# Query and key high/low parts: made at the input projection instead of inside the attention

## The chip, the cores and the metric

The kernel runs on one core of a Trainium2 chip. The metric is the device time of one execution in microseconds (us); the median of several runs is given.

## The reference, cut to what matters

One layer of a hybrid decoder trunk on 512 positions, width 2048. After an RMS norm, one projection `z = a @ w_in` feeds two groups of heads: a gated linear recurrence (RG-LRU) and a sparse attention (NSA) with 16 query heads in 4 key/value groups. Their outputs are normalised, projected by `w_out`, and followed by an MLP and a gated embedding. The part that the change touches:

```
q (512,16,64), k_s and k_w (512,4,64) = columns of z
s = q . k * 64**-0.5 + bias          (selected and window branch, and q . kc for the compressed branch)
p = softmax(s);  o = p . v           (three branches, summed with sigmoid gates)
```

All inputs and outputs are float32.

## The kernel before, in words

**Products in parts.** TensorE multiplies rounded operands (type fp32r). To keep float32 accuracy each operand x is split into a high part h (x rounded, a copy on ScalarE, ACT) and a low part x - h (a subtraction on VectorE, DVE), and a product is three matmuls: high by high, high by low, low by high (`mm3`, L165). The scores take two matmuls, one with the keys' high and one with their low part (L1226, L1227, L1233, L1234). A query tile `al_q` holds for one head the high part of the 64 query dimensions in one half of the 128 partitions and the low part in the other half; the key tiles `kh` and `kl` hold the same 64 dimensions in both halves, so one matmul gives two of the partial products.

**Strips and order.** The work is a list of strips. A strip is 512 columns of a weight tile: four weight blocks of 128 columns, so 12 matmuls. `go` (L188) walks the list once and writes out every engine's instructions in that order: at strip j it makes the high and low part of the weights of strip j + 4 (`split`, lines L159 on ACT and L160 on DVE, from a `raw` buffer that a DMA filled), hands out up to two finished results, and issues the matmuls of strip j. Everything else is hung on a strip position by hand with `at` (in quarters of a strip). Each engine executes its instructions in that order, and so do the DMA issues of each queue: loads are issued by SP, stores by ACT (`store`, L422).

**The input projection** (`front`, L560). 16 pairs of weight tiles in the order kc, vc, k0, k1, 0 to 5, q0, 6, 7, q1, q2, q3. Each pair takes 16 strips (k0 and k1 take eight extra strips of the compression). `proj` (L697) evicts each of the two results of a pair (L701, DVE, 128x512) into a tile `z`; the pairs 0 to 7 stay on chip for the recurrence (`lru_tile`), the others are stored to `z_d` in DRAM, one DMA of 512 KB each. The tiles `z` come from a ring of three buffers (`z_tile`, L241), so a tile waits until the third tile before it has been read. q0 belongs to the heads of group 0, q3 to those of group 3, k0 to groups 0 and 1, k1 to groups 2 and 3.

**The attention** (`mid`, L975; `attention`, L1068; `group`, L1077; `head`, L1206). It runs between the 32 strips of the first half of `w_out`: a step at position s of the attention's own scale is hung at strip b2 + 2 + 0.165 s, where b2 is the first of these strips. Group g starts at B = 11 + 27 g and head r of it at B + 6.75 r; `GA`, `GQ`, `HA`, `HBI` and the like hold the offsets. Before its scores a group prepares:

- `load` (L1087): SP loads the keys twice, into the lower and the upper partitions (L1090, 256 KB each), and the queries (L1092, 512 KB) into two buffers of the `raw` ring of five, which the weight strips use too
- `q_turn` (L1104): DVE scales the queries by -0.125 and reverses the order of positions (L1107, two of 128x512)
- `q_hi`, `q_lo` (L1109, L1113): per head, ACT makes the high part (L1111, 64x512) and DVE the low part (L1115, 64x512)
- `k_hi`, `k_lo` (L1117, L1121): ACT (L1119) and DVE (L1122), 128x1024 each
- `kc_hi`, `kc_lo` (L1124, L1128): the same for the compressed keys, in four small pieces

`c_score` (L1142) is the group's first use of its queries on TensorE (L1145, L1146). In a head, `score(qt)` (L1218) writes into one of two PSUM banks, and `bias(qt)` (L1237, line L1241 on DVE) reads it, adds the bias and takes the minimum, which frees the bank; then follow the exponential (L1246, ACT), a scaling on GpSimd (L1256), transposes (L1266), the split of the transposed probabilities (L1278, L1282) and the products with the values (L1293). The sum of a head is read out by `out_a` and `out_b` (L1308, L1315), which frees the one bank of the output product (L1299).

**At the seam.** `switch2` (L994) reopens the z ring with one buffer, which lies over the buffer that the last tile of the front had used, and clears two constant tiles (`attn_const`, L1061: L1064 and L1066 on DVE). The first results of `w_out` go into that buffer (`y1_out`, L981: L985 on DVE).

Of the kernel before, what the change touches and what calls it, by code (L numbers as in the profile page):

```python
# [9 lines left out]
F32 = mybir.dt.float32  # L10
F32R = mybir.dt.float32r
AF = mybir.ActivationFunctionType
ALU = mybir.AluOpType
AX = mybir.AxisListType

P = 128
S = 512
D = 2048
KT = D // P
DFF = 8192  # L20
LW = 1024
NH = 16
NG = 4
# [11 lines left out]
NTAB = 1039  # L35
# [14 lines left out]
S4 = 4.5  # L50
SX = 8.0
WSA = (-3.5, -2.25, -0.75)
GA = (-11, -10, -7, -5, -5, -4, -4, -0.25, 0.75, 1.75, 2.75, 3.75, 4.75, 6, 6.5, 5.75, 7.75, 8.75, 9.25)
GV = (8.75, 9.75, 10.75)
GQ = (-6, -6, -6, -1.5)
QL = 1.0
HA = (-5, 6.5, 7, 12, 17.5, 18.5)
HSC = (0, 2, 4, 4)
HBI = (1, 3, 5, 5)
# [64 lines left out]
def f32(ap):  # L124
    return ap.bitcast(F32)


def rev(ap):
    dims = [list(d) for d in ap.ap]
    step, n = dims[-1]  # L130
    dims[-1] = [-step, n]
    return bass.AP(tensor=ap.tensor, offset=ap.offset + step * (n - 1), ap=dims)
# [7 lines left out]
class Build:  # L140
# [32 lines left out]
    def at(self, j, fn, *a):  # L173
        key = math.floor(4 * j + 0.5)
        assert self.now is None or key > self.now, (key, self.now)
        self.hooks.setdefault(key, []).append((fn, a))
# [336 lines left out]
    def run(self):  # L513
        tc, nc, A = self.tc, self.nc, self.A
        cp = self.cp = self.pool("const")
        self.wp = self.pool("w")
        self.vec = cp.tile([P, V_N], F32, name="vec")
        self.ident = cp.tile([P, P], F32, name="ident")
        self.ones = cp.tile([P, 1], F32, name="ones")
        nc.vector.memset(self.ones, 1.0)  # L520
        self.scrap = cp.tile([P, 1], F32, name="scrap")
        self.msum = cp.tile([P, S], F32, name="msum")
        self.ps = self.pool("ps", space=bass.MemoryType.PSUM)
        self.rings = {}
        self.direct = ("o", "f")
        dp = self.pool("dram", space=bass.MemoryType.DRAM)
        for nm, shape in (("bv_d", [NH, NTAB]), ("z_d", [16, P, S]), ("y1_d", [KT, P, S]), ("h1_d", [KT, P, S]), 
                          ("f_d", [DFF // P, P, S]), ("pp_d", [KT, P, S])):
            setattr(self, nm, dp.tile(shape, F32, name=nm))
        self.vv_d = dp.tile([NB, P, 8, P], F32, name="vv_d")  # L530
        with tc.high_priority(offset=PRIO), tc.manual_schedule():
            self.front()
            self.mid()
            self.back()
            self.go()
            assert not self.cur
            for nm in ("fbctx", "zctx", "snctx", "yctx", "cyctx", "cxctx"):
                self.T[nm].close()
# [21 lines left out]
    def front(self):  # L560
        nc, A, T, at = self.nc, self.A, self.T, self.at
        v, g, act, pe = nc.vector, nc.gpsimd, nc.scalar, nc.tensor
# [128 lines left out]
        order = ["kc", "vc", "k0", "k1", 0, 1, 2, 3, 4, 5, 6, 7, "q1", "q2", "q3"]  # L691
        order.insert(Q0, "q0")
        mt = {"kc": 0, "vc": 2, "k0": 4, "k1": 6, "q0": 24, "q1": 26, "q2": 28, "q3": 30}
        zr = {"kc": 0, "vc": 2, "k0": 4, "k1": 6, "q0": 8, "q1": 10, "q2": 12, "q3": 14}
        pos = {}

        def proj(nm, r, st):  # L697
            def f(ps):
                if r == 0:
                    st.append(self.z_tile())  # L700
                v.tensor_tensor(st[0][:, r], ps, T["Ra"], op=ALU.mult)  # L701
                if r and nm in mt:
                    self.store(self.z_d[zr[nm]:zr[nm] + 2].rearrange("a p n -> p a n"), st[0])
                elif r:
                    T["lz", nm] = st[0]
            return f

        for nm in order:
            b = pos[nm] = len(self.strips)
            m = mt[nm] if nm in mt else 8 + 2 * nm  # L710
            extra = self.compress(int(nm[1]), b) if nm in ("k0", "k1") else []
            st = []
# [364 lines left out]
    def group(self, g, B, add):  # L1077
        nc, T = self.nc, self.T
        v, po, act, pe = nc.vector, nc.gpsimd, nc.scalar, nc.tensor
        mm = pe.matmul  # L1080
        al, ar = self.al_tile, self.ar_tile
        t, Q = {}, {}
        half = [slice(0, 64), slice(64, 128)]
# [1 line left out]
        cols = [slice(32 * r, 32 * r + NCMP) for r in range(R)]  # L1085

        def load():  # L1087
            t["ka"] = self.raw_tile().rearrange("p (b n) -> p b n", b=2)
            for e in range(2):
                nc.sync.dma_start(t["ka"][half[e]], self.z_d[4 + g].rearrange("(b p) n -> p b n", b=2))  # L1090
            t["qa"] = self.raw_tile().rearrange("p (b n) -> p b n", b=2)
            nc.sync.dma_start(t["qa"], self.z_d[8 + 2 * g:10 + 2 * g].rearrange("a p n -> p a n"))  # L1092

        def load_cmp():
            t["tcb"] = ar("tcb")
# [5 lines left out]
            w = t["vv", n] = ar(f"vv{n}", (P, 2 if n == 1 else 1, 2, P), F32R)  # L1101
            nc.sync.dma_start(f32(w), self.vv_d[ks, :, 2 * g:2 * g + 2].rearrange("t p b d -> p t b d"))

        def q_turn():  # L1104
            t["q"] = self.sum_tile("qt").rearrange("p (a n) -> p a n", a=2)
            for j in range(2):
                v.tensor_scalar(rev(t["q"][:, j]), t["qa"][:, j], -0.125, None, op0=ALU.mult)  # L1107

        def q_hi(h):  # L1109
            Q[h] = al("q", dt=F32R, bufs=4)  # L1110
            act.activation(Q[h][half[h % 2]], t["q"][half[h % 2], h // 2], AF.Copy)  # L1111

        def q_lo(h):  # L1113
            e = h % 2
            v.tensor_tensor(Q[h][half[1 - e]], t["q"][half[e], h // 2], f32(Q[h][half[e]]), op=ALU.subtract)  # L1115

        def k_hi():  # L1117
            t["kh"], t["kl"] = (al(nm, (P, 2, S), F32R, bufs=2) for nm in ("kh", "kl"))
            act.activation(t["kh"], t["ka"], AF.Copy)  # L1119

        def k_lo():  # L1121
            v.tensor_tensor(t["kl"], t["ka"], f32(t["kh"]), op=ALU.subtract)  # L1122

        def kc_hi():  # L1124
            for r in range(R):
# [60 lines left out]
        def c_lo():  # L1186
            v.tensor_tensor(t["pcl"], t["pb"], f32(t["pch"]), op=ALU.subtract)

        for o, fn in zip(GA, (load, load_cmp, q_turn, k_hi, kc_hi, k_lo, kc_lo, c_score, c_bias, c_turn, c_min, c_exp, c_sum,
                              vc_hi, vc_lo, c_norm, c_back, c_hi, c_lo)):  # L1190
            add(B + o, fn)
        for n in range(3):
            add(B + GV[n], lambda n=n: load_v(n))
        for r in range(R):
            o = GQ[r]
            add(B + o, lambda r=r: q_hi(r))
            add(B + o + QL, lambda r=r: q_lo(r))
            self.head(g, r, B + HS * r, add, t, Q)

    def al_tile(self, tag, shape=(P, S), dt=F32, bufs=1):  # L1200
# [568 lines left out]
```

## Time and profile before

| | |
|---|---|
| median of 3 runs | 2378.26 us (2377.45 to 2381.46) |
| the profiled execution | 2378.15 us |
| its span, first to last instruction | 2376.3 us |
| TensorE matmul (PE) busy | 2320.6 us, 98% of the span |
| VectorE (DVE) busy | 1414.8 us, 60% |
| ScalarE (ACT) busy | 1047.4 us, 44% |
| GpSimd (POOL) busy | 111.5 us, 5% |
| mean granted TensorE clock | 0.996 |

The span is one execution on the chip; a sum made from its durations stands against 2378.15 us, of which 1.85 us lie around the span. In the rows, times are in us, `x` gives the number of instructions, PEclk is the granted clock as a share of 2.4 GHz, and a bracket such as `[1.91 <-ACT kcd L1126]` is the engine's idle time just ahead of an instruction and what ended it. Issues of DMAs carry a q after the engine (SPq, ACTq).

### The profile page before, as it was taken

The numbers are of one execution on the slowest core, as the hardware profiler recorded it, in microseconds if no ns is written. First come the engines' busy times: TensorE is split into PE (matmuls) and PEld (weight loads), VectorE is DVE, ScalarE is ACT, GpSimd is POOL, SyncE is SP. The second block draws the span as 40 slices with busy tenths as digits, with TensorE's granted clock in tenths as the row PEclk, the third lists the DMA queues.
The fourth block names the chain that finished last, engine by engine and source line by source line (L and its number), as shares of the span: only waits on it lengthen the run. The fifth ranks groups of instructions, "written<-read, shape, count | busy, mean of one in ns | idle before, by whom it ended". The sixth has DMA issues, their size and how long they took to land.

```text
span 2376.3 us, 33258 instructions
## 1 busy us (share of the span) xinstructions
PE 2320.6 (98%) x12586; PEld 2005.5 (84%) x12586; DVE 1414.8 (60%) x2405; ACT 1047.4 (44%) x1941; POOL 111.5 (5%) x157
## 2 busy tenths in 40 slices
PE   7999999998999999999999999999999999999999
PEld 5788888777788778999999999888888888888887
DVE  6365665488855776888888888433333333334733
ACT  5354665277854553544444444333223223223422
POOL 4000000034410000000000000000000000000000
PEclk9999999999999999999999999999999999999999
DMA  5453233323324553334333335533334333224641
GB/s 190 154 178 109 98 103 108 111 89 94 107 90 144 203 176 124 116 125 136 132 130 129 134 134 170 168 115 133 115 115 133 115 116 133 95 96 138 217 148 69
DMA packets 109604, 308.25 MB, mean 130 GB/s; under 512 B 10914, under 2 KB 16290, under 8 KB 109444
## 3 DMA queue, kind: packets, MB, share of 16 engines
q1 hardware_dynamic: 92532, 270.93, 34.4%
q10 hardware_dynamic: 16912, 35.20, 3.9%
q8 instruction: 98, 1.61, 0.3%
q14 instruction: 62, 0.51, 0.1%
HBM read 266.18 MB, written 39.91 MB: 129 GB/s over the span
## 4 chain that ended last, share of the span: by engine, by line
PE 73%; DVE 4%; ACT 2%; issue 1%; ACTq 0%; POOL 0%; POOLq 0%; DVEq 0%
PE ps_mm L169 23%; PE ps_mm L167 23%; PE ps_mm L168 23%; PE ps_o L1293 1%; PE ps_t L1266 1%; ACT al_P L1246 1%; PE ps_s L1233 0%; DVE slo L160 0%; ACT shi L159 0%; PE ps_s L1234 0%; DVE al_q L1115 0%; DVE y L1425 0%; DVE y L1424 0%; DVE al_pl L1282 0%; PE ps_t L481 0%
## 5 line engine op out<-in xcount | busy, mean ns | idle before, releaser
L160 DVE TENSOR_TENSOR slo<-raw,shi 128x512 fp32r<-128x512 f32 x808 | 559.7, 697 | 807.7 <-ACT shi L159 798.0
L159 ACT ACTIVATE shi<-raw 128x512 fp32r<-128x512 f32 x808 | 504.8, 629 | 921.5 <-PE ps_mm L168 813.3
L167 PE MATMUL ps_mm<-cx,shi 128*128 128x512 f32 (+1 forms) x1984 | 699.7, 353 | 3.8 <-ACT shi L159 1.9
L168 PE MATMUL ps_mm<-cx,shi 128*128 128x512 f32 (+1 forms) x1984 | 696.2, 351 | 3.4 <-DVE cx L1435 3.4
L169 PE MATMUL ps_mm<-cx,slo 128*128 128x512 f32 (+1 forms) x1984 | 696.3, 351 | 0.1
L167 PE MATMUL ps_mm<-cy,shi 128*128 128x512 f32 (+1 forms) x1536 | 543.9, 354 | 2.6 <-ACT shi L159 2.6
L168 PE MATMUL ps_mm<-cy,shi 128*128 128x512 f32 (+1 forms) x1536 | 543.3, 354 | 1.6 <-DVE cy L1435 1.6
L169 PE MATMUL ps_mm<-cy,slo 128*128 128x512 f32 (+1 forms) x1536 | 543.3, 354 | 0.6 <-DVE slo L160 0.6
L167 PEld LDWEIGHTS ps_mm<-cx,shi 128*128 128x128 f32 x1984 | 376.2, 190 | 52.6 <-ACT shi L159 3.1
L168 PEld LDWEIGHTS ps_mm<-cx,shi 128*128 128x128 f32 x1984 | 375.9, 189 | 51.9 <-DVE cx L1435 4.8
L169 PEld LDWEIGHTS ps_mm<-cx,slo 128*128 128x128 f32 x1984 | 375.6, 189 | 51.1 <-DVE slo L160 1.7
L167 PEld LDWEIGHTS ps_mm<-cy,shi 128*128 128x128 f32 x1536 | 290.8, 189 | 42.0 <-ACT shi L159 3.2
L168 PEld LDWEIGHTS ps_mm<-cy,shi 128*128 128x128 f32 x1536 | 290.9, 189 | 41.6 <-DVE cy L1435 2.4
L169 PEld LDWEIGHTS ps_mm<-cy,slo 128*128 128x128 f32 x1536 | 290.8, 189 | 41.2 <-DVE slo L160 1.2
L159 ACT ACTIVATE shi<-wsum 128x512 fp32r<-128x512 f32 x156 | 96.8, 629 | 123.7 <-PE ps_mm L168 73.1
L160 DVE TENSOR_TENSOR slo<-wsum,shi 128x512 fp32r<-128x512 f32 x156 | 106.2, 688 | 36.8 <-ACT shi L159 36.7
L1246 ACT ACTIVATE al_P<-al_P,ar_stm 128x512 f32<-128x512 f32 (+3 forms) x128 | 70.4, 554 | 16.8 <-DVE ar_stm L1241 16.5
L1256 POOL TENSOR_SCALAR al_P<-al_P,ar_sts 128x512 f32<-128x512 f32 (+3 forms) x128 | 74.7, 605 | 63.2 <-ACT al_ph L1278 29.3
L167 PE MATMUL ps_mm<-y,shi 128*128 128x256 f32 x208 | 58.3, 280 | 0.0
L168 PE MATMUL ps_mm<-y,shi 128*128 128x256 f32 x208 | 58.0, 279 | 0.0
L169 PE MATMUL ps_mm<-y,slo 128*128 128x256 f32 x208 | 58.0, 279 | 0.0
L1241 DVE CUSTOM_DVE_ANT_0 al_P<-ps_s,al_tb 128x512 f32<-128x512 f32 (+3 forms) x128 | 56.1, 483 | 1.8 <-PE ps_s L1234 1.5
(347 smaller groups left out, 2017.6 us busy)
## 6 DMA issues: line engine op xcount, KB each, us to landing
raw<-in_mlp_w_dram SPq DMA_DIRECT2D x256, 512.0 KB, 3.6
raw<-in_w_in_dram SPq DMA_DIRECT2D x64, 512.0 KB, 3.6
raw<-in_w_out_dram SPq DMA_DIRECT2D x32, 512.0 KB, 3.7
fk<-f_d SPq DMA_DIRECT2D x32, 512.0 KB, 5.0
raw<-in_ple_gate_dram SPq DMA_DIRECT2D x32, 512.0 KB, 3.7
f_d<-z ACTq DMA_DIRECT2D x26, 512.0 KB, 2.8
y<-in_xT_dram SPq DMA_DIRECT2D x16, 256.0 KB, 6.6
raw<-in_w_v_dram SPq DMA_DIRECT2D x8, 512.0 KB, 5.7
```

The costliest lines, as they stand in the source:

```text
L159: nc.scalar.activation(hi, src, AF.Copy)
L160: (eng or nc.vector).tensor_tensor(lo, src, f32(hi), op=ALU.subtract)
L167: mm(ps, whi, ahi, start=start, stop=False)
L168: mm(ps, whi, alo, start=False, stop=False)
L169: mm(ps, wlo, ahi, start=False, stop=stop)
L1241: v.tensor_tensor_reduce(out=PP[qt, b], in0=X["s", qt][b], in1=X["tb"][:, qt * P:], scale=1.0, scalar=3e38, op0=ALU.add, op1=ALU.min, accu ...
L1246: act.activation(PP[qt, b], PP[qt, b], AF.Exp, scale=-1.0, bias=st["mn"][:, qt, b:b + 1], accum_out=st["sm"][:, qt, b:b + 1])
L1256: pool.tensor_scalar(PP[qt, b], PP[qt, b], st["sm"][:, qt, b:b + 1], 1.0, op0=ALU.mult, op1=ALU.mult)
L1266: pe.transpose(pt[:, qt * P:(qt + 1) * P], PP[qt, b][:, kt * P:(kt + 1) * P], self.ident)
L1293: mm(po[:, :S - kt * P], vv[:, 0, b, :], y, start=False, stop=False)
```

## The change

Queries and keys are split where the input projection evicts them. `split_qk` makes high and low part on 128x1024 tiles (the high part in a further tile `zh` of the ring `z`), a quarter of a strip after the second eviction; the scaling is part of the split, the reversal of positions part of the eviction. `store_qk`, half a strip later, stores the parts to two new DRAM tensors, `q_d` in the layout of the tile `al_q` and `k_d`: two DMAs for a pair of keys, four for a pair of queries, all issued by ACT. The attention loads them ready for TensorE: four DMAs for the keys of a group (`load`), one for each query tile (`load_q`). `q_turn`, `q_hi`, `q_lo`, `k_hi` and `k_lo` are gone. The ring of `al_q` has five buffers in place of four.

```
-GA = (-11, -10, -7, -5, -5, -4, -4, -0.25, 0.75, 1.75, 2.75, 3.75, 4.75, 6, 6.5, 5.75, 7.75, 8.75, 9.25)
+GA = (-11, -10, -5, -4, -0.25, 0.75, 1.75, 2.75, 3.75, 4.75, 6, 6.5, 5.75, 7.75, 8.75, 9.25)
-GQ = (-6, -6, -6, -1.5)
-QL = 1.0
+GQ = (-9.5, -9.25, -9, -8.75)
...
-        for nm, shape in (("bv_d", [NH, NTAB]), ("z_d", [16, P, S]), ("y1_d", [KT, P, S]), ("h1_d", [KT, P, S]), 
+        for nm, shape in (("bv_d", [NH, NTAB]), ("z_d", [4, P, S]), ("y1_d", [KT, P, S]), ("h1_d", [KT, P, S]), 
...
+        self.q_d = dp.tile([NH, P, S], F32, name="q_d")
+        self.k_d = dp.tile([2, NG, P, S], F32, name="k_d")
...
-        zr = {"kc": 0, "vc": 2, "k0": 4, "k1": 6, "q0": 8, "q1": 10, "q2": 12, "q3": 14}
+        zr = {"kc": 0, "vc": 2}
...
+        def split_qk(nm, z):
+            h = self.z_tile("zh").bitcast(F32R)
+            g = int(nm[1])
+            if nm[0] == "q":
+                act.activation(h, z, AF.Copy, scale=-0.125)
+                v.scalar_tensor_tensor(z.bitcast(F32R), z, -0.125, f32(h), op0=ALU.mult, op1=ALU.subtract)
+            else:
+                act.activation(h, z, AF.Copy)
+                v.tensor_tensor(z.bitcast(F32R), z, f32(h), op=ALU.subtract)
+            at(self.now / 4 + 0.5, store_qk, nm[0], g, f32(h), z)
+
+        def store_qk(nm, g, h, z):
+            if nm == "k":
+                for x, t in enumerate((h, z)):
+                    act.dma_start(self.k_d[x, 2 * g:2 * g + 2].rearrange("a p n -> p a n"), t)
+                return
+            for e in range(2):
+                for x, t in enumerate((h, z)):
+                    o = 64 * (e ^ x)
+                    act.dma_start(self.q_d[4 * g + e:4 * g + 4:2, o:o + 64, :].rearrange("a p n -> p a n"),
+                                  t[64 * e:64 * e + 64])
 
         def proj(nm, r, st):
             def f(ps):
                 if r == 0:
                     st.append(self.z_tile())
-                v.tensor_tensor(st[0][:, r], ps, T["Ra"], op=ALU.mult)
-                if r and nm in mt:
+                z = st[0][:, r]
+                v.tensor_tensor(rev(z) if nm in mt and nm[0] == "q" else z, ps, T["Ra"], op=ALU.mult)
+                if r and nm in mt and nm[0] in "qk" and nm != "kc":
+                    at(self.now / 4 + 0.25, split_qk, nm, st[0])
+                elif r and nm in mt:
...
         def load():
-            t["ka"] = self.raw_tile().rearrange("p (b n) -> p b n", b=2)
-            for e in range(2):
-                nc.sync.dma_start(t["ka"][half[e]], self.z_d[4 + g].rearrange("(b p) n -> p b n", b=2))
-            t["qa"] = self.raw_tile().rearrange("p (b n) -> p b n", b=2)
-            nc.sync.dma_start(t["qa"], self.z_d[8 + 2 * g:10 + 2 * g].rearrange("a p n -> p a n"))
+            for x, nm in enumerate(("kh", "kl")):
+                t[nm] = al(nm, (P, 2, S), F32R, bufs=2)
+                for e in range(2):
+                    nc.sync.dma_start(f32(t[nm][half[e]]), self.k_d[x, g].rearrange("(b p) n -> p b n", b=2))
...
-        def q_turn():
...
-        def q_hi(h):
...
-        def q_lo(h):
...
-        def k_hi():
...
-        def k_lo():
...
+        def load_q(h):
+            Q[h] = al("q", dt=F32R, bufs=5)
+            nc.sync.dma_start(f32(Q[h]), self.q_d[4 * g + h])
...
         for r in range(R):
             o = GQ[r]
-            add(B + o, lambda r=r: q_hi(r))
-            add(B + o + QL, lambda r=r: q_lo(r))
+            add(B + o, lambda r=r: load_q(r))
             self.head(g, r, B + HS * r, add, t, Q)
```

## Rows read from the trace of the kernel before

**Rows 1.** Page, part 1: busy time, share of the span, instructions of each engine.

```profile
PE 2320.6 (98%) x12586; PEld 2005.5 (84%) x12586; DVE 1414.8 (60%) x2405; ACT 1047.4 (44%) x1941; POOL 111.5 (5%) x157
```

**Rows 2.** Stretches: length, then busy PE, PEld, DVE, ACT, POOL, clock, DMA share, GB/s.

```profile
300.00:420.00 120.00, 120.00 (x531) 99.19 (x530) 74.10 (x113) 70.99 (x108) 0.00 (x0) 1.00 0.31 104
...
452.00:680.00 228.00, 205.82 (x1123) 171.45 (x1122) 182.95 (x512) 169.32 (x477) 86.93 (x138) 0.97 0.31 93
```

**Rows 3.** Waits of PE over the span: us in total, times, longest us.

```profile
PE ps_o L1299 <- DVE ar_ot L1315: 4.6, 4, 2.4
```

**Rows 4.** Timeline of PE in the attention: start, us, instruction, idle before.

```profile
465.63 0.50 PE L1145 MATMUL ps_t<-al_q,kcd 128*128 128x512 f32 x1 [1.91 <-ACT kcd L1126]
468.47 0.79 PE L1146 MATMUL ps_t<-al_q,kcd 128*128 128x512 f32 x1 [2.34 <-DVE kcd L1130]
...
510.69 0.60 PE L1226 MATMUL ps_s<-al_kh,al_q 128*128 128x512 f32 x1 [2.50 <-DVE ar_stm L1241]
...
519.05 0.47 PE L1145 MATMUL ps_t<-al_q,kcd 128*128 128x512 f32 x1 [1.23 <-DVE al_q L1115]
...
565.15 0.50 PE L1226 MATMUL ps_s<-al_kh,al_q 128*128 128x512 f32 x1 [1.92 <-DVE ar_stm L1241]
...
617.87 0.50 PE L1226 MATMUL ps_s<-al_kh,al_q 128*128 128x512 f32 x1 [2.28 <-DVE ar_stm L1241]
```

**Rows 5.** Timeline of DVE just ahead of the wait at 510.69.

```profile
506.11 2.39 DVE L1115 TENSOR_TENSOR al_q<-qt,al_q 64x512 fp32r<-64x512 f32 x3
508.53 1.23 DVE L1122 TENSOR_TENSOR al_kl<-raw,al_kh 128x1024 fp32r<-128x1024 f32 x1
...
510.07 0.55 DVE L1241 CUSTOM_DVE_ANT_0 al_P<-ps_s,al_tb 128x384 f32<-128x384 f32 x1
```

**Rows 6.** Stretches of lowered clock after three of these waits, columns as in rows 2.

```profile
469.00:474.00 5.00, 5.00 (x14) 3.85 (x13) 2.27 (x5) 0.00 (x0) 0.00 (x0) 0.56 0.00 0
510.00:514.00 4.00, 3.31 (x12) 2.68 (x12) 3.94 (x17) 1.84 (x6) 0.00 (x0) 0.62 0.00 0
565.00:569.00 4.00, 3.85 (x13) 3.17 (x14) 3.94 (x13) 2.14 (x7) 0.00 (x0) 0.57 0.00 0
```

**Rows 7.** Instructions on the tiles qt, al_q, al_kh, al_kl: ns min/median/max, first and last start.

```profile
L1107 DVE TENSOR_SCALAR qt<-raw x8: 420/421/427, 462.1 to 609.1; 128x512 f32<-128x512 f32 x8
...
L1111 ACT ACTIVATE al_q<-qt x16: 627/632/634, 462.6 to 620.2; 64x512 fp32r<-64x512 f32 x16
L1115 DVE TENSOR_TENSOR al_q<-qt,al_q x16: 684/707/1543, 463.2 to 622.0; 64x512 fp32r<-64x512 f32 x16
...
L1119 ACT ACTIVATE al_kh<-raw x4: 1039/1042/1044, 464.4 to 611.7; 128x1024 fp32r<-128x1024 f32 x4
L1122 DVE TENSOR_TENSOR al_kl<-raw,al_kh x4: 1218/1226/1227, 467.1 to 615.7; 128x1024 fp32r<-128x1024 f32 x4
```

**Rows 8.** The same: the gates' eviction, a 128x1024 form, the stores to z_d.

```profile
L634 DVE TENSOR_TENSOR gt<-ps_s,rba x1: 685/685/685, 80.6 to 80.6; 128x512 f32<-128x512 f32 x1
...
L1466 DVE SCALAR_TENSOR_TENSOR z<-z x26: 1224/1225/1227, 987.0 to 1486.7; 128x1024 f32<-128x1024 f32 x26
...
L423 ACTq DMA_DIRECT2D z_d<-z x8: 366/366/391, 100.0 to 455.3; - x8
```

**Rows 9.** DMA issues: queue, count, KB of each, median us from issue to landing.

```profile
z_d<-z ACTq DMA_DIRECT2D x8, 512.0 KB, 4.2
...
raw<-z_d SPq DMA_DIRECT2D x8, 256.0 KB, 4.8
```

**Rows 10.** Timelines of SP and DVE at the seam of front and attention.

```profile
452.00 1.24 SPq L1090 DMA_DIRECT2D raw<-z_d  x2
...
454.61 0.69 DVE L701 TENSOR_TENSOR z<-ps_mm,rba 128x512 f32<-128x512 f32 x1
...
457.64 0.91 DVE L1064 MEMSET kcd<- 128x1024 f32 x1 [0.17 <-DVE slo L160]
...
460.10 0.68 DVE L985 TENSOR_TENSOR z<-ps_mm,rl 128x512 f32<-128x512 f32 x1
```

More of the change, by code (lines that the diff above doesn't have):

```diff
@@ L1102, in load_v @@
             nc.sync.dma_start(f32(w), self.vv_d[ks, :, 2 * g:2 * g + 2].rearrange("t p b d -> p t b d"))
-        def q_turn():
-            t["q"] = self.sum_tile("qt").rearrange("p (a n) -> p a n", a=2)
-            for j in range(2):
-                v.tensor_scalar(rev(t["q"][:, j]), t["qa"][:, j], -0.125, None, op0=ALU.mult)
-        def q_hi(h):
-            Q[h] = al("q", dt=F32R, bufs=4)
-            act.activation(Q[h][half[h % 2]], t["q"][half[h % 2], h // 2], AF.Copy)
-        def q_lo(h):
-            e = h % 2
-            v.tensor_tensor(Q[h][half[1 - e]], t["q"][half[e], h // 2], f32(Q[h][half[e]]), op=ALU.subtract)
-        def k_hi():
-            t["kh"], t["kl"] = (al(nm, (P, 2, S), F32R, bufs=2) for nm in ("kh", "kl"))
-            act.activation(t["kh"], t["ka"], AF.Copy)
-        def k_lo():
-            v.tensor_tensor(t["kl"], t["ka"], f32(t["kh"]), op=ALU.subtract)
+        def load_q(h):
+            Q[h] = al("q", dt=F32R, bufs=5)
+            nc.sync.dma_start(f32(Q[h]), self.q_d[4 * g + h])
         def kc_hi():
@@ L1187, in c_lo @@
             v.tensor_tensor(t["pcl"], t["pb"], f32(t["pch"]), op=ALU.subtract)
-        for o, fn in zip(GA, (load, load_cmp, q_turn, k_hi, kc_hi, k_lo, kc_lo, c_score, c_bias, c_turn, c_min, c_exp, c_sum,
+        for o, fn in zip(GA, (load, load_cmp, kc_hi, kc_lo, c_score, c_bias, c_turn, c_min, c_exp, c_sum,
                               vc_hi, vc_lo, c_norm, c_back, c_hi, c_lo)):
```

## The prediction, made before the changed kernel was built

> **What bounds the kernel now.** The page's first part comes first: TensorE is busy for 98% of the span [rows 1]. So work of another engine counts only where TensorE stands still for it, and the question is where it does. The table of stretches answers that. In the front, from 300 to 420 us, PE is busy for all of 120.00 us, while DVE has 74.1 and ACT 71.0 us of work; from 452 to 680 us, where the attention runs, PE has 205.82 of 228 us, so 22.2 us are idle, and DVE carries 183 us, 80% [rows 2]. The change moves work from the second of these stretches into the first.
>
> Next, the timeline of PE shows where the 22.2 us lie. Six waits belong to the preparation of queries and keys. At the start of the first group PE stands still for 1.91 and 2.34 us, until high and low part of the compressed keys are there; at the starts of the three later groups it waits 2.50, 1.23, 1.92 and 2.28 us [rows 4]. The timeline of DVE says why the wait at 510.69 lasts: 2.39 us of low parts of queries and 1.23 us of low parts of keys stand in DVE's order ahead of the bias step (L1241) that frees the score bank, and PE starts again 0.07 us after the first half of that step, which ends at 510.62 [rows 5]. The waits at 565.15 and 617.87 are the same pattern. The wait at 519.05 is for the low part of the fourth head's query itself. At the start, the compressed keys' parts come behind those of queries and keys, on ACT and on DVE alike.
>
> The six add up to 4.25 us at the start and 7.93 us at the later groups, 12.2 in all. The other 10.0 us lie elsewhere; 4.6 of them in four waits, the longest of 2.4, for the sum of a head to be read out of its bank [rows 3], in which the preparation has no part.
>
> Last, the clock. Behind the waits at 468.47, 510.69 and 565.15 the granted clock stands at 1.2 GHz for a while: its means of 0.56, 0.62 and 0.57 over 5, 4 and 4 us [rows 6] come from 4.4, 3.0 and 3.4 us at half speed, 10.9 us in all. Half of that is lost, 5.4 us: 2.2 at the start, 3.2 at the groups. Behind 617.87 no stretch of this kind is found.
>
> **The change, part by part.** *Removed from the attention:* on DVE 16 low parts of queries at 0.71, four of keys at 1.23 and eight turns at 0.42 us, 19.7 us; on ACT 16 at 0.63 and four at 1.04, 14.3 us [rows 7]. On the path lies only what PE waits for. Take the wait at 510.69: without 3.62 us ahead of it the bias step is 3.6 us earlier, and PE's wait was 2.50, so the bank is free before PE asks. The same holds for 1.92 and 2.28, and the fourth query (1.23) comes ready by DMA. I take the 7.93 us as gone, with 3.2 us of clock. What is late next is the readout of the heads' sums, which the change leaves where it is.
>
> *Added to the front:* for each of six pairs one ACT copy of 128x1024, 1.04 us as for the keys [rows 7], and one DVE subtraction, 1.22 us both for keys and in the form with a scale [rows 7, 8]: 6.3 us on ACT, 7.3 on DVE. Twenty store issues take the place of six: 14 more at 0.37 us [rows 8] are 5.2 us of ACT's queue. I cost all this at nothing. The cover is the lead of four strips with which ACT and DVE prepare weights: 531 matmuls of 12 per strip in 120 us [rows 2] make 2.7 us a strip, so 10.9 us, and one pair's split with its issues takes 1.04 + 1.23 + 4 x 0.37 = 3.7 us. If that cover were gone for every pair, the cost would be 6 x 3.7 = 22 us. The reversal of positions moves from the turns into the eviction L701, which takes 0.69 us [rows 10]; the one eviction of the front that reverses already, L634, takes 0.685 [rows 8], so it adds nothing.
>
> *The wait that is added.* On ACT, the stores of low parts wait for DVE, and the copy of weights for a coming strip stands behind them: at most the 1.23 us of the subtraction, inside the 3.7 above.
>
> *Queues and transfers.* SP issues eight loads per group in place of three. At the first group, four loads of keys at 0.62 us each from 452.0 on [rows 10], four small bias loads (at most the same 0.62) and four queries (I take the 0.37 us of a full-height issue [rows 8]) end by 458.5; with 4.8 us to land [rows 9] all is there by 463.3, and PE wants the first query at 465.63 - 1.91 = 463.7 [rows 4]. This is near, but the key loads need no weight buffer any more and may be issued earlier. In later groups the last query is asked for 8.5 units ahead of `c_score`; 27 units took 52.7 us from 565.15 to 617.87 [rows 4], so 16.6 us. A query load can wait on SP until PE has read the old tile; behind it stand the next bias table and weight loads, due strips later. No cost. Traffic grows by 3 MB of writes and 4 MB of reads, where the attention's DMA share is 0.31 [rows 2]: no cost.
>
> *The seam.* The last pair, q3, is evicted at 454.61, right before the attention. The high part ends at 456.4, the low part at 457.6, the four issues at 458.7. Behind them ACT and DVE have the split of the next strip (0.63 and 0.69: 460.1), DVE the two clears (0.91 and about half that: 461.5) and the next low part (462.2). Then L985, at 460.10 in rows 10, needs the buffer of q3's high part: counting the ring of three through the front, `zh` of q3 is its last tile. The third store, the last that reads it, is issued at 458.0 and, with the 4.2 us of a store to `z_d` [rows 9], frees it at 462.2. L985, a strip's low part and the compressed keys' low parts end at about 464.3, and PE waits 0.6 us where it waited 4.25. So 3.65 us go, and with them, I take it, 2.2 of clock; bounds are nothing (the buffer comes as late as the old wait ended) and 4.25.
>
> **The sum.** 7.93 + 3.65 + 5.4 = 17.0 us. Against it I set new waits: PE reaches the rest of its list earlier, and what it meets there has its own pace. Nothing in this trace gives that price; its ends are 0 and 9.6 us, four new waits like the longest readout of 2.4 us [rows 3]. I take 2.0, half a microsecond per group, nearer to zero, since DVE and ACT lose 5 and 3.6 us of work per group too. So 15 us: 2378.15 - 15.0 = 2363.1 us. The profiled execution lies 0.11 us from the median of the three runs, so no correction is made.
>
> **The rivals.** *1. The seam keeps its wait.* The stores are half-height and issued back to back. If the third needs three times 4.2 us from the first issue, L985 goes at 469.0, what follows it ends 2.1 us later at 471.1, and PE waits 7.4 us, 3.1 more than now. For it: 256 KB halves took 4.8 us each, no less than a full 512 KB store [rows 9]. Against it: that figure was taken with a second half in flight. The time: 2378.15 - 7.93 - 3.2 + 3.1 + 2.0 = 2372.1; with the old 4.25 us kept, 2369.0. The Trainium skill's page "DMA: Bandwidth & Descriptors" (Rules for kernel authors) speaks against halves in just this way: two transfers to disjoint partition halves serialize, and one over 128 partitions should be used. By its fixed 2 us and 436 GB/s three halves would land after an estimated 3.8 us, which would leave my sum as it is.
>
> *2. The waits come back.* PE is as late at the readouts as it was at the group starts: all 9.6 us of new waits and the clock as before, 2378.15 - 11.6 + 9.6 = 2376.2. For it: DVE stays near 80% busy in a shorter stretch. Against: the removed work stood right ahead of the late steps [rows 5].
>
> *3. More goes.* With 20 us less on DVE and 14 on ACT the readouts come in time too: all 22.2 and 5.4 us, 2350.6.
>
> *4. Slower.* The front's cover fails: ACT stands at each pair's stores, weight copies come late, PE runs dry, 22 us: 2378.15 - 15.0 + 22.4 = 2385.5. It decides only if one stop exceeds the 10.9 us of lead; ACT and DVE have 38% or more free there [rows 2].
>
> **How the numbers follow.** The forecast's own range is 2356 to 2369 (the seam's and the new waits' ends, half each): 0.63. Rival 1: 0.13, rival 2: 0.09, rival 3: 0.10, rival 4: 0.05. The range 2353 to 2372.5 holds the forecast and rival 1, and leaves out the most of the others, about 0.2. A measurement here can tell about 0.2%, 4.8 us: faster means under 2373.5. Forecast, rivals 1 and 3 and little of rival 2 give 0.87; the rest of rival 2 gives 0.08 for the same; rival 4 gives 0.05.
>
> **What would show it.** Right: the PE waits at L1145, L1146 and at L1226 ahead of the group starts gone, no lowered clock near them, the front at 120.00 of 120 with 6 to 7 us more on DVE and ACT, the attention near 213 us long, its readout waits still there. Wrong: PE idle before 452 us, a wait of L985 for stores at the seam, a wait for query loads, or new waits that add up to more than 2 us.

## The result, and the profile of the changed kernel

The changed kernel takes **2365.18 us** (median of 5 runs, 2364.17 to 2370.03) where the kernel before takes 2378.26 (5 runs, 2375.99 to 2381.46): a ratio of 0.9949, 95% interval 0.9937 to 0.9961. That is 13.1 us less, inside the range of the prediction and 2.1 us above its number. The profiled execution has a span of 2362.4 us against 2376.3, 13.9 less. Lines are shifted: L725 is the old L701, L961 and L966 the old L935 and L940, L1139 the old L1130, L1154 and L1155 the old L1145 and L1146, L1234 the old L1226, L1307 the old L1299.

The page's first part, the stretches (columns as in rows 2) and one row of PE's waits:

```profile
PE 2316.7 (98%) x12586; PEld 2004.2 (85%) x12586; DVE 1401.7 (59%) x2383; ACT 1039.6 (44%) x1927; POOL 108.5 (5%) x157
```

```profile
120.00:180.00 60.00, 56.81 (x298) 48.29 (x297) 37.41 (x72) 32.03 (x64) 0.00 (x0) 1.00 0.56 181
300.00:420.00 120.00, 120.00 (x530) 99.25 (x529) 72.33 (x109) 72.28 (x109) 0.00 (x0) 1.00 0.35 110
...
452.00:680.00 228.00, 216.26 (x1208) 182.61 (x1207) 172.37 (x501) 164.93 (x472) 83.91 (x138) 0.99 0.40 120
```

```profile
PE ps_o L1307 <- DVE ar_ot L1323: 4.6, 4, 2.4
```

Against rows 2, PE has 10.4 us less idle time between 452 and 680 us, and the front from 300 to 420 us is still full. The readout waits are the old ones to the digit shown [rows 3]. But in 120 to 180 us PE lacks 3.2 us. PE's timeline shows the single waits; first two rows of the kernel before that stand at the edges of the attention's gain:

```profile
154.84 0.43 PE L940 MATMUL ps_t<-ident,cz 124*128 124x124 f32 x2 [0.90 <-DVE cz L935]
...
675.67 0.33 PE L1266 MATMUL ps_t<-ident,al_P 128*128 128x128 f32 x1 [0.45 <-POOL al_P L1256]
```

and the rows of the changed kernel:

```profile
156.76 0.43 PE L966 MATMUL ps_t<-ident,cz 124*128 124x124 f32 x2 [3.19 <-DVE cz L961]
...
465.87 0.47 PE L1154 MATMUL ps_t<-al_q,kcd 128*128 128x512 f32 x1 [0.23 <-DMA al_q<-q_d]
466.65 0.50 PE L1155 MATMUL ps_t<-al_q,kcd 128*128 128x512 f32 x1 [0.31 <-DVE kcd L1139]
...
469.78 0.47 PE L1154 MATMUL ps_t<-al_q,kcd 128*128 128x512 f32 x1 [1.70 <-DMA al_q<-q_d]
...
661.69 0.33 PE L1274 MATMUL ps_t<-ident,al_P 128*128 128x128 f32 x1 [0.45 <-POOL al_P L1264]
```

Three things are to be seen. The four waits at the starts of the later groups (7.93 us, rows 4) have no row any more. At the seam 2.24 us of idle time are left of 4.25, and 1.93 of them now wait for **a query load**, a kind of wait that was not there before. And at 156.76, in the front, a wait of 0.90 us has become 3.19. No clock is lost behind the seam (first row), but the changed kernel has a lowered stretch of its own (second row), behind its readout wait of 2.21 us at 643.18; the kernel before had the full clock behind the same wait of 2.20 us at 658.75:

```profile
469.00:474.00 5.00, 4.22 (x22) 3.66 (x23) 3.37 (x8) 2.09 (x3) 0.00 (x0) 1.00 0.42 164
...
640.00:650.00 10.00, 7.79 (x35) 6.32 (x34) 6.32 (x21) 5.98 (x18) 4.10 (x8) 0.83 0.01 2
```

The account of the spans: the changed kernel is 1.92 us *late* at the transpose of the front (156.76 - 154.84; 2.29 of longer wait, less 0.37 that it was early before) and 13.98 us *early* at 661.69, which was at 675.67. So the attention gives 15.9 us: 7.93 of waits at the groups, 2.01 at the seam, half a microsecond of smaller waits, and 5.5 by which PE is busy for less time with the same work (498.65 us before, 493.19 now, between these two instructions). I put the 5.5 down to the clock; the exact share is not shown, since the changed kernel loses 1.7 us of clock in the stretch above. The front takes 2.3 back.

Of the prediction's signs for being right, the waits at L1226 ahead of the groups are gone with the full clock there, 300 to 420 us is full and the readouts stayed; at L1145 and L1146 waits remain. Two of its signs for being wrong came as well: PE idle before 452 us for longer than in the kernel before, and a wait for query loads. DVE and ACT got 4.9 and 3.9 us more up to 452 us, where 6 to 7 were expected for the whole front; q3's split lies behind that time.

**Where the two costs come from.** First the front: ACT and then DVE, right after the second eviction of k0.

```profile
150.89 1.06 ACT L705 ACTIVATE zh<-z 128x1024 fp32r<-128x1024 f32 x1 [1.44 <-DVE z L725]
151.98 0.37 ACTq L712 DMA_DIRECT2D k_d<-zh  x1
153.24 0.37 ACTq L712 DMA_DIRECT2D k_d<-z  x1
...
154.19 0.37 ACT L955 ACTIVATE cz<-ps_s 124x256 f32<-124x256 f32 x1
```

```profile
151.98 1.23 DVE L706 TENSOR_TENSOR z<-z,zh 128x1024 fp32r<-128x1024 f32 x1 [1.12 <-ACT zh L705]
...
156.28 0.43 DVE L961 SCALAR_TENSOR_TENSOR cz<-cz 124x256 f32<-124x256 f32 x1 [0.15 <-ACT cz L959]
```

The split of k0 with its two stores stands ahead of the token compression's gelu (L955 to L961), and PE's transpose waits for the gelu's last step. Then the seam: ACT's queue with the four stores of q3, and SP's queue with the four query loads of group 0.

```profile
458.34 0.60 ACTq L717 DMA_DIRECT2D q_d<-zh  x1
459.60 0.74 ACTq L717 DMA_DIRECT2D q_d<-z  x1
460.38 0.62 ACTq L717 DMA_DIRECT2D q_d<-zh  x1
461.04 0.70 ACTq L717 DMA_DIRECT2D q_d<-z  x1
461.79 1.15 ACT L158 ACTIVATE shi<-raw 128x512 fp32r<-128x512 f32 x2 [3.48 <-DMA q_d<-zh]
```

```profile
454.56 2.95 SPq L1122 DMA_DIRECT2D ar_tcb<-bv_d  x4
461.41 0.34 SPq L1131 DMA_DIRECT2D al_q<-q_d  x1
462.96 0.34 SPq L1131 DMA_DIRECT2D al_q<-q_d  x1
464.01 0.32 SPq L1131 DMA_DIRECT2D al_q<-q_d  x1
465.50 0.32 SPq L1131 DMA_DIRECT2D al_q<-q_d  x1
```

SP is done with the bias loads at 457.51 and then stands until 461.41, though what the first load reads is q0's, stored long before. Its four loads go out 3.07, 3.36, 3.63 and 4.46 us after q3's four stores, one by one.

### The profile page after: what moved, and what is told of

It reads as the page before. It is cut to its first block, busy times and chain, and to the rows that moved or that the text cites. A ratio compares the mean times of both kernels' runs of the same rounds, so it can differ in the third digit from the quotient of the medians.

```text
span 2362.4 us, 33256 instructions
## 1 busy us (share of the span) xinstructions
PE 2316.7 (98%) x12586; PEld 2004.2 (85%) x12586; DVE 1401.7 (59%) x2383; ACT 1039.6 (44%) x1927; POOL 108.5 (5%) x157
## 4 chain that ended last, share of the span: by engine, by line
PE 90%; DVE 4%; ACT 2%; DMA 2%; issue 1%; ACTq 0%; SPq 0%; POOL 0%; POOLq 0%; DVEq 0%
PE ps_mm L166 28%; PE ps_mm L168 27%; PE ps_mm L167 27%; PE ps_o L1301 1%; PE ps_t L1274 1%; DVE slo L159 1%; PE ps_s L1241 1%; DMA y<-in_xT_dram 1%; ACT shi L158 1%; PE ps_s L1242 0%; PE ps_mm L615 0%; ACT al_P L1254 0%; PE ps_mm L616 0%; PE ps_mm L614 0%; PE ps_t L480 0%
## 5 line engine op out<-in xcount | busy, mean ns | idle before, releaser
L1249 DVE CUSTOM_DVE_ANT_0 al_P<-ps_s,al_tb 128x512 f32<-128x512 f32 (+3 forms) x128 | 56.1, 483 | 2.7 <-POOL al_P L1264 1.6
```

Source lines behind the costliest of these rows:

```text
L1249: v.tensor_tensor_reduce(out=PP[qt, b], in0=X["s", qt][b], in1=X["tb"][:, qt * P:], scale=1.0, scalar=3e38, op0=ALU.add, op1=ALU.min, accu ...
```

## The experiments

Eight kernels, all edits of the changed one; in the two halves (6 and 7) the part left out is as in the kernel before. Where an edit makes dummy work, nothing reads its result. The kernel before was run again beside them, with a median of 2376.72 us beside 1, 2, 4 and 5 and of 2378.08 beside 3, 6, 7 and 8; the ratios are to these. Only the intervals of 4 and 7 stand clear of the changed kernel's (0.9937 to 0.9961). For the others a difference in the time alone decides little, and the trace is the evidence.

**1. k0's split later.**

```diff
-                    at(self.now / 4 + 0.25, split_qk, nm, st[0])
+                    at(self.now / 4 + (6.25 if nm == "k0" else 0.25), split_qk, nm, st[0])
```

> The changed kernel, with the split of k0 (ScalarE's copy into z, VectorE's low part, and the two stores of each half) put 6.25 strips after its eviction and not 0.25; nothing else differs. Theory: those pieces stand ahead of the gelu that VectorE and ScalarE do for the token compression, and that is why TensorE's wait at the transpose of L966 is 3.19 us where it was 0.90. Expected: that wait back at 0.9 to 1.2 us, TensorE busy 59 us of the stretch 120 to 180, and the time 2 to 2.5 us less than the changed kernel's 2365.2, near 2363. Rival: the wait comes from elsewhere in the front (DRAM traffic of the stores, a later load): it stays near 3.2 us and the time stays within 0.5 us.

Measured: 2363.13 us (5 runs; ratio to the kernel before 0.9936, 0.9923 to 0.9948), 2.05 less than the changed kernel. The stretch of the front:

```profile
120.00:180.00 60.00, 60.00 (x313) 51.15 (x312) 38.94 (x73) 33.08 (x66) 0.00 (x0) 1.00 0.60 195
```

PE is busy throughout, so the wait is gone altogether, better than the 0.9 of the kernel before. There the store of k0 still stood ahead of the gelu on ACT, and ACT waited with it for the eviction of k0, as ACT's row behind that store in the kernel before shows; here nothing stands ahead.

```profile
151.73 0.63 ACT L159 ACTIVATE shi<-raw 128x512 fp32r<-128x512 f32 x1 [1.93 <-DVE z L701]
```

The cost in the front is the place of this one split.

**2. Group 0's query loads first.**

```diff
-            add(B + o, lambda r=r: load_q(r))
+            add(B + (o if g else -11.25), lambda r=r: load_q(r))
```

> The changed kernel, with the four query loads of group 0 issued ahead of the group's key and bias loads on SP instead of behind them. Theory (a completion counter is used again): each load waits, before it is issued, until the transfer that used its counter last has landed, and for the query loads these are q3's stores, whatever they read. Then the order on SP does not help: three of the loads still stand behind q3's stores, now with the keys behind them, so TensorE's idle time at the seam (2.24 us in the changed kernel) stays or grows, up to 5 us, and the time is 0 to 3 us more. Rival (SP's queue was only busy with keys and bias): the query loads issue 3 us earlier or more, the seam's idle time falls to some 0.5 us, and the time falls by about 1.7 us.

Measured: 2363.70 us (4 runs; 0.9944, 0.9930 to 0.9957), 1.5 less than the changed kernel. SP's query loads and PE's only wait at the seam:

```profile
448.23 3.29 SPq L1131 DMA_DIRECT2D al_q<-q_d  x4
```

```profile
466.00 0.50 PE L1155 MATMUL ps_t<-al_q,kcd 128*128 128x512 f32 x1 [0.81 <-DVE kcd L1139]
```

The rival's numbers came: the loads go out 13 us earlier and the seam's idle time falls from 2.24 to 0.81 us. My expectation had the order wrong: at this place the loads are written out *ahead of* q3's stores, so by either theory nothing of q3 holds them. The run shows the cost and its cure, but not why the loads stood behind the stores in the changed kernel. The next one tests one reason, and the compiled program gives the other.

**3. Each group's queries in a tensor of its own.**

```diff
-        self.q_d = dp.tile([NH, P, S], F32, name="q_d")
+        self.q_d = [dp.tile([4, P, S], F32, name=f"q{g}_d") for g in range(4)]
```

> The changed kernel with each group's queries in a DRAM tensor of their own, so that group 0's loads and q3's stores share no tensor; the order of the work is unchanged. Theory (the loads wait because they use the completion counters that q3's four stores used last): the four loads still issue one by one, each 3 to 4.5 us after one of q3's stores was issued, TensorE's idle time at the seam stays at 2.2 us within 0.4 us, and the time stays. Rival (they wait because loads and stores share the tensor q_d): the loads issue right behind the bias loads, 4 us earlier, and the seam's idle time falls below 1 us.

Measured in one execution: 2365.74 us. ACT's stores of q3 and SP's loads:

```profile
459.82 0.60 ACTq L717 DMA_DIRECT2D q_d<-zh  x1
461.08 0.90 ACTq L717 DMA_DIRECT2D q_d<-z  x1
462.03 0.62 ACTq L717 DMA_DIRECT2D q_d<-zh  x1
462.69 0.70 ACTq L717 DMA_DIRECT2D q_d<-z  x1
```

```profile
463.12 0.34 SPq L1131 DMA_DIRECT2D al_q<-q_d  x1
464.60 0.34 SPq L1131 DMA_DIRECT2D al_q<-q_d  x1
465.68 0.32 SPq L1131 DMA_DIRECT2D al_q<-q_d  x1
467.17 0.32 SPq L1131 DMA_DIRECT2D al_q<-q_d  x1
```

The loads still follow the stores one by one, 3.30 to 4.48 us after each, and the seam's idle time is 2.5 us (0.49, 0.21 and 1.80). So it is not the shared tensor. What is left is what the compiled program itself says: the DMAs of SP and ACT share eight completion counters, a transfer adds 16 to its counter, and a DMA that takes a counter is held until that counter's last user has landed. In the changed kernel (head and half put into words):

```
queue  DMA                          held until         counts on
ACT    q_d (q3, first)   <- zh      counter 4 at 320   counter 4
ACT    q_d (q3, second)  <- z       counter 5 at 320   counter 5
ACT    q_d (q3, third)   <- zh      counter 6 at 320   counter 6
ACT    q_d (q3, fourth)  <- z       counter 7 at 320   counter 7
SP     al_q <- q_d (q0, head 0)     counter 4 at 336   counter 4
SP     al_q <- q_d (q0, head 1)     counter 5 at 336   counter 5
SP     al_q <- q_d (q0, head 2)     counter 6 at 336   counter 6
SP     al_q <- q_d (q0, head 3)     counter 7 at 336   counter 7
```

The program of this experiment has the same holds. In that of experiment 2 the four loads use the counters 0 to 3, last used by a weight load and by the first three of q2's stores, and are held by those.

**4. VectorE's work put back.** For groups 1 to 3:

```diff
+        def dve_q():
+            t["x"] = self.sum_tile("scr")
+            for r in range(3):
+                v.tensor_tensor(t["x"][half[0], :S], f32(t["kh"][half[0], 0]), f32(t["kl"][half[0], 0]), op=ALU.subtract)
+        def dve_k():
+            v.tensor_tensor(t["x"].rearrange("p (a n) -> p a n", a=2), f32(t["kh"]), f32(t["kl"]), op=ALU.subtract)
+        if g:
+            add(B - 5, dve_q)
+            add(B - 4, dve_k)
```

> The changed kernel, with the load on VectorE that the splits were in the attention put back for groups 1 to 3 as dummy work at the old places of the order: three subtractions of 64x512 and one of 128x1024 per group, into a tile that nothing reads. Theory (VectorE's queue made TensorE wait at the later groups, and the waits lowered the clock): TensorE's waits at the starts of groups 1 to 3 come back, some 5 to 7 us together, and the granted clock falls below 0.7 behind them, 2 to 3 us more, so the time rises by 6 to 10 us, to 2371 to 2375. Rival (the waits went because the queries and keys no longer pass the raw tiles, or because ScalarE got free): no waits, time within 1 us of the changed kernel's.

Measured: 2375.12 us (10 runs; 0.9992, 0.9983 to 1.0001). The whole gain is gone in the time. PE's timeline (L1246 is L1234 of the changed kernel, L1319 is L1307) and the clock behind the three waits:

```profile
510.02 0.50 PE L1246 MATMUL ps_s<-al_kh,al_q 128*128 128x512 f32 x1 [2.02 <-DVE ar_stm L1261]
...
562.47 0.50 PE L1246 MATMUL ps_s<-al_kh,al_q 128*128 128x512 f32 x1 [1.37 <-DVE ar_stm L1261]
565.48 0.50 PE L1319 MATMUL ps_o<-al_pch,vcb 128*128 128x512 f32 x1 [0.89 <-DVE ar_ot L1335]
...
613.47 0.50 PE L1246 MATMUL ps_s<-al_kh,al_q 128*128 128x512 f32 x1 [2.17 <-DVE ar_stm L1261]
```

```profile
510.00:515.00 5.00, 4.98 (x27) 4.12 (x28) 4.94 (x16) 4.62 (x14) 0.00 (x0) 1.00 0.13 38
562.00:570.00 8.00, 6.64 (x34) 5.34 (x35) 7.00 (x22) 5.98 (x19) 2.82 (x3) 1.00 0.26 53
613.00:618.00 5.00, 4.53 (x16) 3.69 (x17) 4.46 (x16) 4.40 (x15) 1.28 (x1) 0.66 0.09 15
```

The dummy work took 4.0, 4.1 and 3.4 us of DVE in the three groups, where the splits took 3.62 [rows 5], so it is near to them and not the same. With queries and keys loaded ready as in the changed kernel it brings back 2.02, 1.37 and 2.17 us of the old 2.50, 1.92 and 2.28, at the same places. The clock fell behind the third of these waits only, not behind all as expected. The waits don't explain all of the time: in the profiled execution, 11.7 us longer than the changed kernel's, nearly half is lowered clock, and most of that lies behind waits that the changed kernel has too (see the last section). A cheap operation costs when it stands ahead of the one step that frees a bank.

**5. ScalarE's work put back**, in the same way: three `activation(..., AF.Copy)` of 64x512 at B - 6 and one of 128x1024 at B - 5.

> The changed kernel, with ScalarE's part of the splits put back for groups 1 to 3 as dummy work at the old places: three copies of 64x512 and one of 128x1024 per group, into a tile that nothing reads. Theory (VectorE, not ScalarE, was the late engine): no new TensorE wait over 0.5 us at the starts of groups 1 to 3, the clock stays at 1.00, and the time rises by 0 to 1.5 us. Rival (ScalarE's exponentials were held up, and these the readouts): waits of 1 to 2.5 us come back at the starts of the groups and the time rises by 4 us or more.

Measured: 2368.75 us (4 runs; 0.9958, 0.9943 to 0.9973), 3.6 above the changed kernel, more than the 1.5 expected. At the starts of the groups there is no wait; the timeline has one new one, 0.42 us at a readout. The profiled execution's span is 5.3 us longer than the changed kernel's, and the clock explains 5.1 of them. Four stretches, of 1.7 us lost each, are lowered here and not in the changed kernel's profile: 0.72 over 6 us behind L966, 0.66 over 5 us at the seam, 0.66 from 850 to 855 us, and this one behind the readout wait of 2.41 us that every one of these kernels has. The one behind 643.18 is lowered only there.

```profile
538.00:543.00 5.00, 4.40 (x17) 3.91 (x18) 3.98 (x15) 3.53 (x12) 2.71 (x3) 0.67 0.38 109
```

So ACT was not the late engine. That its work costs some time in another way, by the clock for one, stays open, since the intervals of the two kernels overlap.

**6. Only the queries moved.** The keys are stored whole and split by the attention as before (ACT at B - 5, DVE at B - 4).

> Half of the change: the queries' parts are made at the input projection and loaded ready, the keys are kept whole in DRAM and split by the attention as in the kernel before (ScalarE's copy 5 strips and VectorE's low part of 1.23 us 4 strips ahead of each group). Theory (the waits at the later groups are VectorE's time, and the queries were some two thirds of it): TensorE waits at those starts for at most 0.5 us each with the clock at 1.00, the wait at L966's transpose is back at 0.9 us because k0 is not split there, and the time is 2363 to 2366. Rival (any work of VectorE there is too late): waits of 1 to 1.5 us come back at each of the three later groups, the clock falls behind them, and the time is 2368 to 2371.

Measured: 2361.98 us (4 runs; 0.9938, 0.9922 to 0.9954). PE's rows in the front and at the seam (L1164 is L1155 of the changed kernel):

```profile
154.60 0.43 PE L966 MATMUL ps_t<-ident,cz 124*128 124x124 f32 x2 [0.94 <-DVE cz L961]
...
465.70 0.50 PE L1164 MATMUL ps_t<-al_q,kcd 128*128 128x512 f32 x1 [1.53 <-DVE kcd L1148]
```

No wait at the starts of the later groups, 0.94 in the front, and a time a little below the range expected. Half of the change gives all of the gain and pays none of the front's cost; at the seam 1.73 us are left of 4.25, 1.53 of them for the compressed keys' low part and not for query loads. In this profile the clock is full from 100 to 800 us, which is 1.7 us of its lead over the changed kernel's.

**7. Only the keys moved.** The queries go through the attention as before.

> The other half: the keys' parts are made at the input projection and loaded ready, the queries go through the attention as in the kernel before (turned on VectorE, copied on ScalarE, low parts on VectorE). Theory: 1.23 us of VectorE is off each group, so the three waits of 2.50, 1.92 and 2.28 us fall to about 1.3, 0.7 and 1.0 us and the fourth of 1.23 us stays; the seam keeps about 4 us; the 2.3 us at L966's transpose are paid as in the changed kernel; the time is 2371 to 2375 where the kernel before has 2377. Rival (keys carry most of the gain): the waits vanish and the time is under 2368.

Measured: 2371.18 us (9 runs; 0.9974, 0.9964 to 0.9983). PE's timeline (L1249 is L1234 of the changed kernel, L1168 and L1169 are L1154 and L1155):

```profile
468.51 0.50 PE L1169 MATMUL ps_t<-al_q,kcd 128*128 128x512 f32 x1 [1.02 <-DVE kcd L1153]
...
507.25 0.50 PE L1249 MATMUL ps_s<-al_kh,al_q 128*128 128x512 f32 x1 [1.34 <-DVE ar_stm L1264]
514.16 0.47 PE L1168 MATMUL ps_t<-al_q,kcd 128*128 128x512 f32 x1 [1.36 <-DVE al_q L1143]
...
559.12 0.50 PE L1249 MATMUL ps_s<-al_kh,al_q 128*128 128x512 f32 x1 [0.77 <-DVE ar_stm L1264]
...
609.66 0.50 PE L1249 MATMUL ps_s<-al_kh,al_q 128*128 128x512 f32 x1 [1.30 <-DVE ar_stm L1264]
```

The waits are the old ones less the keys' 1.23 us, within 0.25: 1.34, 0.77 and 1.30 for 1.27, 0.69 and 1.05, and the fourth stays. Such subtraction works as long as the wait is longer than what is taken away. At the seam the expectation was wrong: 1.02 us of idle time are left (first row), not about 4. So the keys alone free most of the seam, with the queries split there as before; why was not followed further.

**8. Both orders mended**, the edits of 1 and 2 together.

> The changed kernel with both orders mended: k0's split 6.25 strips after its eviction, and the query loads of group 0 ahead of its key and bias loads. Theory (the two costs stand in different stretches and add): TensorE's wait at L966 at 0.9 us or less, and the seam's at about 0.8 us, for VectorE's kcd alone; 3.5 to 4 us less than the changed kernel, 2361 to 2362 against 2377 for the kernel before, a ratio of 0.9930 to 0.9937. Rival (one of the gains is taken back by a wait further on): 2363 to 2364.

Measured: **2360.51 us** (5 runs, 2359.54 to 2361.54; 0.9927, 0.9913 to 0.9942), 17.6 us below the kernel before and 4.7 below the changed one. The seam's only wait:

```profile
463.36 0.50 PE L1155 MATMUL ps_t<-al_q,kcd 128*128 128x512 f32 x1 [0.80 <-DVE kcd L1139]
```

The two gains add in the trace: PE is full from 120 to 180 us as in 1, and the seam is that of 2. By its median this is the fastest of the kernels here, and all five runs lie below all of the changed kernel's; its interval overlaps those of 1, 2 and 6 and, by a little, the changed kernel's.

## Why the prediction was right, and which of its steps were not

**The waits at the groups (7.93 us): right, and shown.** Taken as gone because DVE's 3.62 us ahead of the bias step exceed each wait, they are gone; experiment 4 brings them back with DVE's work alone, 5 does not with ACT's. The prediction didn't see that the queries' part suffices (experiment 6).

**New waits (2.0 us set against the sum): none came.** "What is late next is the readout" holds in the sense that its waits stayed, 4.6 us in four. They did not grow.

**The clock (5.4 us): the size came, as 5.5 us less of busy time, but it is no fixed sum.** None of the three stretches of rows 6 is left, and a new one has come, behind the wait at 643.18. That the total fits is in part luck: as the last section shows, the same wait is followed by either level.

**"I cost all this at nothing": wrong by 2.3 us.** The cover it named, the lead of four strips of weights, held where it was read, from 300 to 420 us. A split with its issues took ACT 2.7 us for the keys k0 (150.89 to 153.61) and 4.5 us for the queries q3 (457.25 to 461.74), where 3.7 was worked out. The step that failed is that one stretch spoke for the whole front. At k0 another chain without that lead, the compression's gelu, stands behind the split on both engines and PE waits for it. So something like rival 4 came about, at one pair of six and at a tenth of its price; but what came late was the gelu, not the weight copies that the rival named.

**"Four queries ... end by 458.5": wrong, the last was issued at 465.50.** The step counted how long SP takes to issue, not what holds an issue. Instead each load stood behind the landing of one of q3's stores (experiments 2 and 3). The stores' issue was also mis-sized: 0.60 to 0.74 us for a half-height store, not the 0.37 of the full-height one, so that ACT was held 3.48 us. The half-height loads of rows 10 had taken 0.62 each already.

**The seam (3.65 us): 2.01 came.** Its remaining wait was put at 0.6 us for the compressed keys' low part. That term measured 0.31, and 0.80 or 0.81 where the queries are there in time (experiments 2 and 8). The other 1.93 us are the query loads. L1011 (L985 before), which was to wait for a buffer, ran without a wait in its row.

**Rival 1** had the right place and the wrong mechanism: the seam kept a wait, but no store held up L1011. If a load's issue marks the landing of the store before it at the latest, the third store had landed at 464.01, 5.7 us after the first issue; the rival had it at three times 4.2. The halves did land one behind the other, 1.0 to 1.6 us apart. The rule of the Trainium skill's page "DMA: Bandwidth & Descriptors" (Rules for kernel authors), that halves serialize, is not contradicted by this. The estimate of 3.8 us made from the page's figures was short of the 5.7; the page gives these figures for DMAs issued from GpSimd, and these stores were issued by ACT.

So the attention gave 15.9 us where the sum had 15.0: the 2.0 set against it didn't come, the seam gave 1.64 less, smaller waits half a microsecond more. The front, set at zero, took 2.3. The number came out well because the allowance for new waits, which weren't there, stood in for a cost that was; that part is luck.

## What to carry to other kernels

Work moved to an engine that is 60% busy is free only if no short chain that TensorE waits for stands right behind it in the order: look at each place where the moved work lands, not at one stretch's busy time. A load may be held by a store that it has nothing to do with, if both count on the same counter; so write early loads out ahead of late stores, and read in the trace whether an idle DMA queue starts again when some other transfer lands. And try each half of a change alone: by the medians the queries alone gave 16.1 us, the keys alone 6.9 and both together 13.1. What the two take away overlaps, and the keys' split adds its cost in the front.

## What was not expected of the hardware

The granted clock behind one and the same wait is not the same in all these profiles, one execution of each kernel. The readout wait of 2.4 us is in all ten kernels at the same place of the work; behind it the clock fell in five profiles and stayed full in five. It was full in the changed kernel (first row) and 0.66 with the query loads first (second row, another kernel, same wait):

```profile
534.00:539.00 5.00, 4.23 (x24) 3.73 (x25) 3.97 (x15) 4.02 (x13) 2.55 (x3) 1.00 0.33 70
```

```profile
532.00:537.00 5.00, 4.83 (x20) 4.33 (x21) 3.89 (x15) 3.53 (x12) 3.14 (x4) 0.66 0.50 127
```

The wait of 3.2 us at L966 likewise: 1.00 behind it in the changed kernel, 0.72 over 156 to 162 us in experiment 3. A mean of 0.66 over 5 us between levels of 1.2 and 2.4 GHz is 3.4 us at the lower one and 1.7 us lost. So a clock term read from one profiled execution is a sample; what decides between the levels stays open, and so does whether a kernel's own edit has a part in it. The changed kernel's five runs spread over 5.9 us. Their mean granted clocks go the same way, 0.997 in the fastest and 0.994 in the slowest, and three thousandths of the span are 7 us; so the clock may be most of that spread, which was not tested further.
